# MLP up projection in passes of 512 and 256 columns, block pairs emptied together, partial sums combined in the last group

## The chip, the cores and the metric

The kernel runs on one core of a Trainium2 chip. The metric is the time of one execution on the device in microseconds (us). TensorE is called PE here, VectorE DVE, ScalarE ACT, GpSimd POOL and SyncE SP.

## What is computed

The reference is a trunk of two layers over 256 positions of width 2048, in float32. Each layer adds an attention mixer and an MLP to the residual stream; the change is in the MLP:

```python
def squared_relu_mlp(h, w_up, w_down):
    return jnp.square(jax.nn.relu(h @ w_up)) @ w_down

for layer in range(DEPTH):
    ...
    h = rms_norm(x, mlp_norm[layer])
    x = x + squared_relu_mlp(h, w_up[layer], w_down[layer]).astype(x.dtype)
```

`w_up` is 2048 x 8192 and `w_down` 8192 x 2048.

## The kernel before

Every weight is multiplied in two parts, `hi` (rounded to the matmul's type) and `lo` (the rest); the moving or stationary activations have such parts too, and a product takes three matmuls: hi with hi, hi with lo, lo with hi.

All weights pass through one list, `stream`, of chunks of 128 x 1024 (some 128 x 512). SP loads `raw` tiles of 1 MB (three buffers), ACT copies a chunk to `hi` (L1276, five buffers), DVE makes `lo` = raw - hi (L1284, four buffers), and PE uses both. The main loop does, for chunk i: issue `hi` up to i + 4, `lo` up to i + 3, the matmuls of chunk i, and then a tick of `Jobs`, a list of generators that issue the work beside the stream; a job asks at each `yield` for the tick of its next step. Every engine runs its own instructions in the order in which this loop issues them, so the loop's order is each engine's queue. A tick follows an up or down chunk, and the second chunk of a pair of product chunks.

An MLP (`mlp`) has eight groups of 1024 hidden columns. The up projection of a group is four blocks of 256 columns, each of four chunks: a step (one of 16 k tiles, one half of the block) is three 256-wide matmuls into the PSUM tile `up` (L463 to L465). `up_done` empties a block: Relu from PSUM (L1000), Square into `hr` (L1002), and, as a job one tick later, four sums and differences (L1011 to L1014), ACT's copy into `hs` (L1015) and DVE's rest (L1016), the seven operands of a Strassen product.

The down projection of groups 0 to 6 is done as seven products (L496 to L498) into the PSUM tiles `s0` and `s1`. A unit of 1 MB gives four chunks: a plain one, a single one of half the size, and two that DVE prepares first, w13 (L1043) and w24 (L1049, L1050). Per group there are 32 such chunks, and two of them go with one up chunk of the next group. `products_done` copies the seven sums to `stage` (L1072), and POOL adds them to `sums` in DRAM (L1077). After group 6, `combine` loads them back (L1085), adds them (L1090 to L1095), scales them (L1098), transposes them on PE (L1105) and adds them to the residual `xT` (L1106). The last group's down projection is plain: eight blocks of two chunks (L472, L473), emptied by a copy and three DVE instructions (`down_done`, L1127 to L1131).

Small PE results (transposes, norms) go to `side`, two PSUM banks kept through the whole program.

## Time and profile before

| | |
|---|---|
| median of 3 runs | 2223.57 us (2222.49 to 2226.78) |
| the profiled execution | 2223.32 us, span 2221.5 us |
| PE busy | 2156.0 us (97% of the span) |
| DVE busy | 1745.0 us (79%) |
| ACT busy | 1316.7 us (59%) |
| mean granted PE clock | 0.987 |

The span runs from the first to the last instruction; the execution's time has 1.8 us around it. Matmuls overlap: a row of 0.28 us is followed by the next after some 0.12 us, so the rate is read from the number of matmuls in a stretch, and not from the length of one. "Busy" counts a stretch in which at least one is under way. A granted clock of 1.00 is 2.4 GHz, and 0.50 is 1.2 GHz. The first MLP runs from 361 to 1095 us of the span, the second from 1470 to the end.

### The profile page before, as it was taken

How to read it: one execution, taken by the hardware profiler on the slowest of the kernel's cores; microseconds unless marked ns; L12 is line 12 of the kernel's file. 1: busy time of each engine (PE TensorE's matmuls, PEld its weight loads, DVE VectorE, ACT ScalarE, POOL GpSimd, SP SyncE). 2: the span in 40 equal slices, each digit the busy share in tenths (PEclk: the TensorE clock that was granted, in tenths of full speed). 3: DMA queues.
4: the chain of work that ended last, by engine and by line, in shares of the span. 5: the costliest groups of instructions: out<-in, count | busy, mean ns of one | idle time of the engine just before them, and what ended most of it. 6: DMA issues, size and time to landing. Idle time of an engine off the chain costs nothing.

```text
span 2221.5 us, 39419 instructions
## 1 busy us (share of the span) xinstructions
PE 2156.0 (97%) x16086; PEld 2058.3 (93%) x16086; DVE 1745.0 (79%) x2248; ACT 1316.7 (59%) x1777; POOL 108.9 (5%) x144
## 2 busy tenths in 40 slices
PE   9999999999999999978999999999999999999787
PEld 7898989999999999978888899899999999999776
DVE  6765666898999999977966665568898999999766
ACT  6554545566667666655655446455666666666553
POOL 0000000000000000000000000000000000000000
PEclk9999999999999999999999999999999999999898
DMA  8545456577888888877554456565778888888772
GB/s 264 171 148 161 152 188 177 183 248 216 239 229 246 232 240 240 238 218 227 175 171 136 154 185 191 147 191 179 250 223 241 229 242 235 240 239 233 210 230 83
DMA packets 297685, 455.51 MB, mean 205 GB/s; under 512 B 10696, under 2 KB 172560, under 8 KB 297376
## 3 DMA queue, kind: packets, MB, share of 16 engines
q1 hardware_dynamic: 280224, 392.32, 56.0%
q0 software_dynamic: 17248, 60.67, 13.0%
q8 instruction: 126, 2.06, 0.4%
q14 instruction: 55, 0.45, 0.1%
q10 hardware_dynamic: 32, 0.01, 0.0%
HBM read 399.49 MB, written 53.48 MB: 204 GB/s over the span
## 4 chain that ended last, share of the span: by engine, by line
issue 26%; PE 20%; DMA 2%; POOL 2%; DVE 2%; ACT 1%; POOLq 0%; ACTq 0%; DVEq 0%; SPq 0%
PE mm L472 7%; PE mm L473 4%; POOL sums L1077 2%; PE mm L457 1%; PE mm L458 1%; PE mm L459 1%; DMA sums<-stage 1%; DMA hs<-sums 1%; PE up L463 1%; PE up L464 1%; PE up L465 1%; DVE lo L1284 1%; PE side L350 1%; DMA raw<-w_up 1%; PE mm L475 1%
## 5 line engine op out<-in xcount | busy, mean ns | idle before, releaser
L1284 DVE TENSOR_TENSOR lo<-raw,hi 128x1024 fp32r<-128x1024 f32 (+1 forms) x756 | 825.1, 1113 | 189.2 <-PE mm L473 74.9
L1276 ACT ACTIVATE hi<-raw 128x1024 fp32r<-128x1024 f32 (+1 forms) x756 | 717.9, 966 | 413.8 <-DMA raw<-w_up 169.2
L465 PE MATMUL up<-xs,lo 128*128 128x256 f32 x2048 | 579.6, 283 | 6.6 <-DVE lo L1284 6.2
L463 PE MATMUL up<-xs,hi 128*128 128x256 f32 x2048 | 578.8, 283 | 1.6 <-DVE xT L757 1.6
L464 PE MATMUL up<-xs,hi 128*128 128x256 f32 x2048 | 579.0, 283 | 0.0
L496 PE MATMUL s<-hi,hs 128*128 128x256 f32 x1568 | 445.7, 284 | 0.0
L497 PE MATMUL s<-lo,hs 128*128 128x256 f32 x1568 | 444.1, 283 | 0.0
L498 PE MATMUL s<-hi,hs 128*128 128x256 f32 x1568 | 443.7, 283 | 0.0
L465 PEld LDWEIGHTS up<-xs,lo 128*128 128x128 f32 x2048 | 387.8, 189 | 12.0 <-DVE lo L1284 11.2
L463 PEld LDWEIGHTS up<-xs,hi 128*128 128x128 f32 x2048 | 385.2, 188 | 1.9 <-ACT hi L1276 1.9
L464 PEld LDWEIGHTS up<-xs,hi 128*128 128x128 f32 x2048 | 385.0, 188 | 0.0
L472 PE MATMUL mm<-xs,hi 128*128 128x512 f32 x885 | 319.5, 401 | 0.4 <-ACT hi L1276 0.4
L1276 ACT ACTIVATE hi<-w 128x1024 fp32r<-128x1024 f32 x224 | 236.1, 1054 | 130.3 <-DVE w L1050 85.6
L496 PEld LDWEIGHTS s<-hi,hs 128*128 128x128 f32 x1568 | 300.1, 191 | 0.0
L497 PEld LDWEIGHTS s<-lo,hs 128*128 128x128 f32 x1568 | 300.1, 191 | 0.0
L498 PEld LDWEIGHTS s<-hi,hs 128*128 128x128 f32 x1568 | 299.5, 191 | 0.0
L1284 DVE TENSOR_TENSOR lo<-w,hi 128x1024 fp32r<-128x1024 f32 x224 | 273.8, 1222 | 24.2 <-ACT hi L1276 18.9
L473 PE MATMUL mm<-xs,lo 128*128 128x256 f32 x944 | 259.3, 280 | 0.2 <-DVE lo L1284 0.2
L472 PEld LDWEIGHTS mm<-xs,hi 128*128 128x128 f32 x885 | 166.1, 188 | 38.1 <-ACT hi L1276 0.9
L473 PEld LDWEIGHTS mm<-xs,lo 128*128 128x128 f32 x944 | 177.5, 188 | 3.0 <-DVE lo L1284 0.5
L1043 DVE TENSOR_TENSOR w<-raw 128x1024 f32<-128x1024 f32 x112 | 136.4, 1218 | 0.0
L1077 POOL DMA_DIRECT2D sums<-stage x96 | 82.9, 863 | 973.0 <-ACT stage L1072 955.8
(302 smaller groups left out, 2669.9 us busy)
## 6 DMA issues: line engine op xcount, KB each, us to landing
raw<-w_up SPq DMA_DIRECT2D x128, 1024.0 KB, 5.8
raw<-w_down SPq DMA_DIRECT2D x128, 1024.0 KB, 6.4
raw<-od_w_in SPq DMA_DIRECT2D x36, 1024.0 KB, 5.0
raw<-ev_w_in SPq DMA_DIRECT2D x30, 1024.0 KB, 5.3
sums<-stage POOLq DMA_DIRECT2D x56, 512.0 KB, 6.1
sums<-stage POOLq DMA_DIRECT2D x56, 384.0 KB, 6.4
raw<-ev_w_out SPq DMA_DIRECT2D x16, 1024.0 KB, 5.0
raw<-od_w_in SPq DMA_DIRECT2D x20, 512.0 KB, 4.4
```

The costliest lines, as they stand in the source:

```text
L463: mm(ps[:, j], hi[:, n, c], m[:, 0:T], start=first and j == 0, stop=False)
L464: mm(ps[:, j], hi[:, n, c], m[:, T:], start=False, stop=False)
L465: mm(ps[:, j], lo[:, n, c], m[:, 0:T], start=False, stop=last and j == 1)
L472: mm(ps[:, j], hi[:, n, c], m, start=first, stop=False)
L473: mm(ps[:, j, 0:T], lo[:, n, c], m[:, 0:T], start=False, stop=False)
L496: mm(ps, x[:, a, 0:P], hi[:, o, q], start=first and at % 2 == 0, stop=False)
L497: mm(ps, x[:, a, 0:P], lo[:, o, q], start=False, stop=False)
L498: mm(ps, x[:, a, P:], hi[:, o, q], start=False, stop=last and (at % 2 == 1 or prod == 3))
L1043: tt(four(t), w[:, :, :, 1].rearrange("p q k c -> p k q c"), w[:, :, 0].rearrange("p q h c -> p h q c"), op=OP.subtract)
L1077: nc.gpsimd.dma_start(to, stage, accum_op=OP.add)
L1276: act(d, r, AF.Copy)
L1284: tt(d, r, f32(h), op=OP.subtract)
```

## The change

- A step of the up projection is one 512-wide matmul of `hi` with both parts of the activations, and one 256-wide of `lo`, as in the mixers. The block has a PSUM tile of two banks; ACT copies the second half out, and DVE adds the first to it, ahead of Relu.
- Up weights are loaded 512 columns wide, four k tiles at a time; two blocks share a load and alternate chunk by chunk.
- The two blocks of a pair have one `hr` and one `hs` tile. The four sums, the copy and the rest are issued once for both, the sums in the tick of the second block, the copy and the rest one tick later.
- The up projection runs 18 chunks ahead of the products instead of 16; the last two pairs of product chunks have no up chunk behind them.
- All four `combine` start when the last product is done, and their transposes stand between the blocks of the last down projection.
- The two `side` banks are kept by the mixers alone. In an MLP such results go to halves of `s0` and `s1`, and later of `up`. The final norm's gain is loaded late, into the tiles of w13 and w24.

```diff
     def side():
-        return psum.tile([P, 512], F32, name="side", bufs=2)
+        return st["side"]()
...
     def open_banks(pool_ctx, name):
-        st["banks"] = pool_ctx.enter_context(
+        pool = st["banks"] = pool_ctx.enter_context(
             tc.tile_pool(name=name, bufs=1, space=bass.MemoryType.PSUM, reuse_waits="tile"))
+        st["side"] = lambda: pool.tile([P, 512], F32, name="side", bufs=2)
...
             c = slice(j * P, (j + 1) * P)
-            if block.kind == "U":
-                mm(ps[:, j], hi[:, n, c], m[:, 0:T], start=first and j == 0, stop=False)
-                mm(ps[:, j], hi[:, n, c], m[:, T:], start=False, stop=False)
-                mm(ps[:, j], lo[:, n, c], m[:, 0:T], start=False, stop=last and j == 1)
-            elif block.kind == "last":
+            if block.kind == "last":
...
         def open_pool():
             open_banks(pool_ctx, f"mlp{layer}_ps")
+            turn = [0]
+
+            def free_half():
+                turn[0] ^= 1
+                return banks(f"s{turn[0]}", 1)[:, 0]
+            st["side"] = free_half
             E["pool"] = pool_ctx.enter_context(tc.tile_pool(name=f"mlp{layer}", bufs=1, reuse_waits="tile"))
-            if last:
-                fn = E["fn"] = E["pool"].tile([P, D], F32, name="fn")
-                nc.gpsimd.dma_start(fn, final_norm.unsqueeze(0).to_broadcast([P, D]))
+
+        def load_gain():
+            fn = [E["pool"].tile([P, D // 2], F32, name=n) for n in ("w13", "w24")]
+            for i in range(2):
+                c = slice(i * D // 2, (i + 1) * D // 2)
+                nc.gpsimd.dma_start(fn[i], final_norm[c].unsqueeze(0).to_broadcast([P, D // 2]))
+            E["fn"] = lambda c0, n: fn[c0 // (D // 2)][:, c0 % (D // 2):c0 % (D // 2) + n]
...
         def take_up():
-            return st["banks"].tile([P, 2, T], F32, name="up", bufs=2)
+            return banks("up", 2)
         def take_down(b):
             return lambda: banks(f"s{b % 2}", 1)
         def take_last():
-            two = [take_up(), take_up()]
-            return [t[:, 0] for t in two]
+            ps = banks("s1", 1)
+            return [ps[:, j, 0:T] for j in range(2)]
         def up_done(grp, b):
             def f(ps):
                 t = temp()
-                act(t, ps, AF.Relu)
-                r = E["pool"].tile([P, 8, P], F32, name="hr", bufs=1)
-                act(r[:, 0:4].rearrange("p (j k) t -> p j (k t)", j=2), t, AF.Square)
-
-                def job():
-                    h = E["pool"].tile([P, 7, 2 * P], F32R, name="hs", bufs=2 * nb)
-                    if grp == NGRP - 1:
-                        h = h.rearrange("p o t -> p (o t)")[:, 0:4 * T].rearrange("p (j t) -> p j t", j=2)
-                        split_into(h, r[:, 0:4].rearrange("p (j k) t -> p j (k t)", j=2))
-                    else:
-
-                        tt(r[:, 4], r[:, 0], r[:, 2], op=OP.add)
-                        tt(r[:, 6], r[:, 1], r[:, 0], op=OP.subtract)
-                        tt(r[:, 5], r[:, 4], r[:, 1], op=OP.subtract)
-                        tt(r[:, 7], r[:, 3], r[:, 5], op=OP.subtract)
-                        act(h[:, :, 0:P], r[:, 1:8], AF.Copy)
-                        tt(h[:, :, P:], r[:, 1:8], f32(h[:, :, 0:P]), op=OP.subtract)
-                    hs[grp, b] = h
-                    jobs.done.add(("h", layer, grp, b))
+                act(t, ps[:, :, T:], AF.Copy)
+                tt(t, ps[:, :, 0:T], t, op=OP.add)
+                act(t, t, AF.Relu)
+                if b % 2 == 0:
+                    E["r"] = E["pool"].tile([P, 2, 8, P], F32, name="hr", bufs=1)
+                r = E["r"]
+                act(r[:, b % 2, 0:4].rearrange("p (j k) t -> p j (k t)", j=2), t, AF.Square)
+                if b % 2:
+                    jobs.spawn(job(r), keys=[("h", layer, grp, i) for i in (b - 1, b)], delay=0)
+
+            def job(r):
+                h = E["pool"].tile([P, 2, 7, 2 * P], F32R, name="hs", bufs=nb)
+                if grp == NGRP - 1:
                     yield 1, 0
-                jobs.spawn(job(), keys=[("h", layer, grp, b)], delay=1)
+                    for i in range(2):
+                        hi = h[:, i].rearrange("p o t -> p (o t)")[:, 0:4 * T].rearrange("p (j t) -> p j t", j=2)
+                        split_into(hi, r[:, i, 0:4].rearrange("p (j k) t -> p j (k t)", j=2))
+                        hs[grp, b - 1 + i] = hi
+                else:
+
+                    tt(r[:, :, 4], r[:, :, 0], r[:, :, 2], op=OP.add)
+                    tt(r[:, :, 6], r[:, :, 1], r[:, :, 0], op=OP.subtract)
+                    tt(r[:, :, 5], r[:, :, 4], r[:, :, 1], op=OP.subtract)
+                    tt(r[:, :, 7], r[:, :, 3], r[:, :, 5], op=OP.subtract)
+                    yield 1, 0
+                    act(h[:, :, :, 0:P], r[:, :, 1:8], AF.Copy)
+                    tt(h[:, :, :, P:], r[:, :, 1:8], f32(h[:, :, :, 0:P]), op=OP.subtract)
+                    for i in range(2):
+                        hs[grp, b - 1 + i] = h[:, i]
+                for i in range(2):
+                    jobs.done.add(("h", layer, grp, b - 1 + i))
+                yield 1, 0
             return f
...
-                if grp == NGRP - 2 and half == "s1":
-                    jobs.spawn(combine(cb), keys=[("sum", cb)], delay=1)
+                if grp == NGRP - 2 and half == "s1" and cb == 3:
+                    st["side"] = lambda: banks("up", 2)[:, 0]
+                    for i in range(4):
+                        jobs.spawn(combine(i), keys=[("sum", i)], delay=i)
+                    if last:
+                        load_gain()
             return f
         def combine(cb):
-            s = E["pool"].tile([P, 7, 2 * P], F32, name="hs", bufs=2 * nb)
+            if cb % 2 == 0:
+                E["s"] = E["pool"].tile([P, 2, 7, 2 * P], F32, name="hs", bufs=nb)
+            s = E["s"][:, cb % 2]
             nc.gpsimd.dma_start(s, sums[cb].rearrange("p (o c) -> p o c", o=7))
-            yield 3, 0
...
-            r = E.setdefault("r", st["r"])
+            r = E.setdefault("rms", st["r"])
             for tok in range(2):
                 act(g[:, tok], g[:, tok], AF.Copy, scale=r[:, tok:tok + 1])
-            yield 1, 1
+            yield 2, 1
...
         def up_list(grp):
-            blocks = [Block("U", eights(up, grp * W + b * T, KT), mov, up_done(grp, b), take=take_up)
-                      for b in range(nb)]
-            return [(block, i) for block in blocks for i in range(len(block.chunks))]
+            order = []
+            for b in range(0, nb, 2):
+                c = w_chunks(up, grp * W + b * T, fours(KT))
+                two = [Block("T", c[i], mov, up_done(grp, b + i), take=take_up) for i in range(2)]
+                order += [(block, i) for i in range(len(c[0])) for block in two]
+            return order
...
-        stream.extend(up_list(0))
-        for grp in range(NGRP - 1):
-            s, u = product_list(grp), up_list(grp + 1)
-            for i in range(len(u)):
-                stream.extend(s[2 * i:2 * i + 2] + u[i:i + 1])
+        ups = [c for grp in range(NGRP) for c in up_list(grp)]
+        prods = [c for grp in range(NGRP - 1) for c in product_list(grp)]
+        lead = KT // 4 * nb + 2
+        stream.extend(ups[:lead])
+        for i in range(len(prods) // 2):
+            stream.extend(prods[2 * i:2 * i + 2] + ups[lead + i:lead + i + 1])
```

How the rows move on the engines is shown at the end of an up block (DVE, ACT) and in the last groups (PE). First DVE at the end of an up block beside products, before: the block's last matmul was issued just ahead of the row of w24 with L1049, and `lo` rows from there are the chunks of w13, of w24, of the next up chunk and of the plain and single chunks behind it.

```order
L1049 TENSOR_TENSOR w24_8304<-w13_8270,raw_8080 128x512 [waits DVE_49]
L1050 TENSOR_TENSOR w24_8304<-raw_8080,w24_8304 128x512 [waits DVE_49]
L1284 TENSOR_TENSOR lo_8308<-w13_8270,hi_8269 128x1024 [waits PE_49,Activation_49]
L1284 TENSOR_TENSOR lo_8325<-w24_8304,hi_8303 128x1024 [waits PE_49,Activation_49]
L1011 TENSOR_TENSOR hr_8301<-hr_8301 128x128
L1012 TENSOR_TENSOR hr_8301<-hr_8301 128x128
L1013 TENSOR_TENSOR hr_8301<-hr_8301 128x128 [waits DVE_49]
L1014 TENSOR_TENSOR hr_8301<-hr_8301 128x128 [waits DVE_49]
L1016 TENSOR_TENSOR hs_8335<-hr_8301,hs_8335 128x7x128 [waits Activation_49]
L1284 TENSOR_TENSOR lo_8344<-raw_8193,hi_8323 128x1024 [waits PE_49]
```

DVE had no row in emptying the block, and its sums follow the `lo` of w13 and w24 by a tick. DVE now, from the end of the second block of a pair on:

```order
L1007 TENSOR_TENSOR t_8008<-up_7654,t_8008 128x512 [waits Activation_49]
L1026 TENSOR_TENSOR hr_7951<-hr_7951 128x2x128 [waits Activation_49]
L1027 TENSOR_TENSOR hr_7951<-hr_7951 128x2x128
L1028 TENSOR_TENSOR hr_7951<-hr_7951 128x2x128 [waits DVE_49]
L1029 TENSOR_TENSOR hr_7951<-hr_7951 128x2x128 [waits DVE_49]
L1066 TENSOR_TENSOR w24_8019<-w13_7987,raw_7818 128x512
L1067 TENSOR_TENSOR w24_8019<-raw_7818,w24_8019 128x512 [waits DVE_49]
L1311 TENSOR_TENSOR lo_8023<-w13_7987,hi_7986 128x1024
L1311 TENSOR_TENSOR lo_8039<-w24_8019,hi_8018 128x1024 [waits PE_49,Activation_49]
L1032 TENSOR_TENSOR hs_8013<-hr_7951,hs_8013 128x14x128 [waits Activation_49]
L1311 TENSOR_TENSOR lo_8056<-raw_7917,hi_8037 128x1024 [waits PE_49]
```

The add of the block (L1007) and the four sums of the pair (L1026 to L1029) now stand ahead of w24 and of the `lo` of w13; the `hs` row is twice as long and comes, as before, between the `lo` of w24 and that of the next up chunk.

ACT now, at the same place (L1006 is the new copy out of PSUM, L1008 Relu, L1012 Square, L1031 the copy for both blocks):

```order
L1006 ACTIVATE t_8008<-up_7654 128x512 [waits PE_49]
L1008 ACTIVATE t_8008<-t_8008 128x512 [waits DVE_49]
L1012 ACTIVATE hr_7951<-t_8008 128x512 [waits Activation_49]
L1303 ACTIVATE hi_8018<-w24_8019 128x1024 [waits DVE_49]
L1303 ACTIVATE hi_8037<-raw_7917 128x1024 [waits PE_49]
L1089 ACTIVATE stage_8049<-s0_7900 128x768 [waits DMASW5_49,PE_49]
L1031 ACTIVATE hs_8013<-hr_7951 128x14x128 [waits Activation_49]
```

Relu waits for DVE's add, the `hi` of w24 stands behind Square and waits for DVE's w24, and the stage copy stands ahead of the long copy.

The second place is PE in the last groups of an MLP. Before, the first transposes of a `combine` (here the first of layer 1) stand behind an up chunk, with products to follow:

```order
L464 MATMUL up<-xs,hi 128x256
L465 MATMUL up<-xs,lo 128x256
L1105 MATMUL side<-misc,hr 128x128 x4
L496 MATMUL s_22729<-hi,hs 128x256
L497 MATMUL s_22729<-lo,hs 128x256
```

Now they stand behind the third block of the last down projection:

```order
L469 MATMUL s_21473<-hs,lo 128x256
L471 MATMUL s_21473<-hs,hi 128x512
L1128 MATMUL up<-misc,hr 128x128 x4
L468 MATMUL s_21538<-hs,hi 128x512
L469 MATMUL s_21538<-hs,lo 128x256
```

They have moved behind all products and six down chunks, and write to a tile of `up`.

## Rows read from the trace of the kernel before

**Rows 1.** The page: busy us (share of the span) and instructions.

```profile
PE 2156.0 (97%) x16086; PEld 2058.3 (93%) x16086; DVE 1745.0 (79%) x2248; ACT 1316.7 (59%) x1777; POOL 108.9 (5%) x144
```

**Rows 2.** Stretches: us, busy us (x instructions) by engine, PEclk, DMA, GB/s.

```profile
300.00:330.00 30.00, 30.00 (x173) 26.14 (x173) 18.52 (x21) 14.02 (x17) 0.00 (x0) 1.00 0.61 201
669.00:930.00 261.00, 260.88 (x2182) 260.19 (x2181) 239.11 (x279) 177.92 (x207) 20.71 (x24) 1.00 0.85 238
```

**Rows 3.** Stretches at the end of the two MLPs, same columns.

```profile
952.00:1042.00 90.00, 73.73 (x564) 72.35 (x563) 66.35 (x81) 48.66 (x58) 7.69 (x10) 0.91 0.72 210
2066.00:2151.00 85.00, 66.23 (x507) 64.72 (x507) 60.64 (x74) 42.66 (x50) 6.35 (x9) 0.88 0.68 199
```

**Rows 4.** The waits of PE: total us, times, longest.

```profile
PE side L1105 <- ACT hr L1098: 43.1, 9, 7.6
PE up L465 <- DVE lo L1284: 6.2, 13, 1.6
```

**Rows 5.** Timeline of DVE at a block's end: start, us, instruction, idle before.

```profile
800.92 0.69 DVE L1049 TENSOR_TENSOR w<-w,raw 128x512 f32<-128x512 f32 x1
...
802.25 1.22 DVE L1284 TENSOR_TENSOR lo<-w,hi 128x1024 fp32r<-128x1024 f32 x1
803.74 1.23 DVE L1284 TENSOR_TENSOR lo<-w,hi 128x1024 fp32r<-128x1024 f32 x1 [0.28 <-ACT hi L1276]
804.89 0.28 DVE L1011 TENSOR_TENSOR hr<-hr 128x128 f32<-128x128 f32 x1
805.09 0.28 DVE L1012 TENSOR_TENSOR hr<-hr 128x128 f32<-128x128 f32 x1
...
805.61 0.29 DVE L1014 TENSOR_TENSOR hr<-hr 128x128 f32<-128x128 f32 x1
806.98 1.09 DVE L1016 TENSOR_TENSOR hs<-hr,hs 128x896 fp32r<-128x896 f32 x1 [1.08 <-ACT hs L1015]
807.99 1.22 DVE L1284 TENSOR_TENSOR lo<-raw,hi 128x1024 fp32r<-128x1024 f32 x1
```

**Rows 6.** Timeline of ACT at the same place.

```profile
801.50 0.59 ACT L1000 ACTIVATE t<-up 128x512 f32<-128x512 f32 x1
802.12 0.64 ACT L1002 ACTIVATE hr<-t 128x512 f32<-128x512 f32 x1
802.66 1.04 ACT L1276 ACTIVATE hi<-w 128x1024 fp32r<-128x1024 f32 x1
...
805.99 0.95 ACT L1015 ACTIVATE hs<-hr 128x896 fp32r<-128x896 f32 x1 [1.34 <-DVE hr L1014]
```

**Rows 7.** Timeline of PE at the same place.

```profile
801.24 0.28 PE L496 MATMUL s<-hi,hs 128*128 128x256 f32 x1
...
803.38 0.28 PE L463 MATMUL up<-xs,hi 128*128 128x256 f32 x1
...
806.25 0.28 PE L496 MATMUL s<-hi,hs 128*128 128x256 f32 x1
```

**Rows 8.** The tile up: count, ns min/median/max, first and last start.

```profile
L465 PE MATMUL up<-xs,lo x2048: 274/282/389, 361.4 to 2151.8; 128*128 128x256 f32 x187
...
L1207 DVE TENSOR_TENSOR t<-up,rB x2: 414/415/416, 2209.0 to 2209.8; 128x256 f32<-128x256 f32 x2
```

**Rows 9.** A stretch of layer 0's last stage, columns as in 2.

```profile
1072.00:1078.00 6.00, 6.00 (x37) 5.24 (x36) 5.93 (x10) 4.21 (x8) 0.00 (x0) 1.00 0.68 220
```

**Rows 10.** The page, DMA issues: count, KB each, us to landing.

```profile
sums<-stage POOLq DMA_DIRECT2D x56, 384.0 KB, 6.4
```

**Rows 11.** Groups of ACT by form: busy us, mean ns, idle before.

```profile
L1072 ACT ACTIVATE stage<-s 128x768 f32<-128x768 f32 x56 | 44.4, 792 | 0.0
```

**Rows 12.** Timeline of PE before a combine's transpose in layer 0.

```profile
1028.76 0.33 PE L1105 MATMUL side<-misc,hr 128*128 128x128 f32 x1 [3.65 <-ACT hr L1098]
```

**Rows 13.** Stretches around an idle of PE, columns as in 2.

```profile
545.00:548.40 3.40, 1.87 (x16) 1.67 (x15) 2.32 (x4) 2.42 (x3) 0.00 (x0) 1.00 0.85 258
1029.00:1033.00 4.00, 3.72 (x20) 3.63 (x20) 3.81 (x6) 1.84 (x3) 0.00 (x0) 0.57 0.02 4
```

More of the change, by code (lines that the diff above doesn't have):

```diff
@@ L142, in trunk @@
     tmp = ctx.enter_context(tc.tile_pool(name="tmp", bufs=1))
-    psum = ctx.enter_context(tc.tile_pool(name="psum", bufs=1, space=bass.MemoryType.PSUM))
     dram = ctx.enter_context(tc.tile_pool(name="dram", bufs=1, space=bass.MemoryType.DRAM))
@@ L1077, in f @@
                     nc.gpsimd.dma_start(to, stage, accum_op=OP.add)
[L1078 to L1079 removed]
+                if grp == NGRP - 2 and half == "s1" and cb == 3:
[4 more added lines that the diff above has]
+                        load_gain()
             return f
         def combine(cb):
[L1084 removed]
+            if cb % 2 == 0:
+                E["s"] = E["pool"].tile([P, 2, 7, 2 * P], F32, name="hs", bufs=nb)
+            s = E["s"][:, cb % 2]
             nc.gpsimd.dma_start(s, sums[cb].rearrange("p (o c) -> p o c", o=7))
[L1086 removed]
+            yield 4 + cb, 0
             p1, p2, p3, p5, p7, p6, p4 = (s[:, i] for i in range(7))
@@ L1195, in job @@
                     nc.tensor.transpose(pv[:, tok, j * P:(j + 1) * P], xT[b][:, j, tok * P:(tok + 1) * P], ident)
-            fn = E["fn"][:, b * T:(b + 1) * T]
+            fn = E["fn"](b * T, T)
             tt(st["o"][:, :, b * T:(b + 1) * T], pv, fn[:, None, :].to_broadcast([P, 2, T]), op=OP.mult)
@@ L1209, in last_block @@
             act(sq[:, j], xl[:, j], AF.Square)
-        sums, turn = banks("s1", 1), side()
+        sums, turn = banks("s0", 1), side()
         def add_up(a, first, last):
@@ L1220, in turn_out @@
             tt(o[:, :, c0:c0 + P], turn[:, j * T:(j + 1) * T].rearrange("p (t c) -> p t c", c=P),
-               E["fn"][:, None, c0:c0 + P].to_broadcast([P, 2, P]), op=OP.mult)
+               E["fn"](c0, P)[:, None].to_broadcast([P, 2, P]), op=OP.mult)
         add_up(acc[:, 0], True, False)
```

## The prediction

> **What bounds the kernel now.** I read the engines' busy times first, then stretches of the span, then single instructions around the one place that the change touches most. PE is busy for 2156.0 us of the span and DVE for 1745.0 us [rows 1], so any gain has to come out of PE's own work or its idle time. The stretches say where there is idle time. In the steady part of the first MLP PE is busy 260.88 of 261 us, and 2182 matmuls in that time are 119.6 ns each; DVE is busy 239.11 us (92%) beside it [rows 2]. At the end of each MLP, while the partial sums come back, PE is busy only 73.73 of 90 us and 66.23 of 85 us, at a mean granted clock of 0.91 and 0.88 [rows 3]. All of the kernel's long PE idles stand there: nine waits of the transposes of `combine`, 43.1 us, against 6.2 us in thirteen waits for a `lo` in the up projection [rows 4].
>
> The third view is the end of one up block in that steady part [rows 5 to 7]. Call T the start of the matmul behind the block's last one, 801.24. PE then has a plain and a single product chunk (to 803.38, 2.14 us), an up chunk (to 806.25, 2.87 us), the chunks of w13 and w24 (24 matmuls, 2.87 us) and the next up chunk, whose first `lo` matmul it reaches at about 809.12 + 0.24 = 809.36. DVE meanwhile makes the `lo` of w13 (802.25) and w24 (803.74), four `hr` sums, waits 1.08 us for ACT's copy, makes `hs` (806.98) and then the `lo` of that up chunk, from 807.99 to 809.21. It is done 0.15 us ahead of PE. **PE loses nothing there, but the cover is used up**: whatever is put into DVE's queue between T and that `lo` is paid by PE. That is what the change does.
>
> **The change part by part.** *Matmuls of the up projection.* 2048 steps of three 256-wide matmuls [rows 8] become one of 512 and one of 256. Three cost 3 x 119.6 = 359 ns. The pair stands in the first output projection: 173 matmuls in 30 us [rows 2], 347 ns a pair. 12 ns x 2048 = **24 us less**. The Trainium skill (TensorE: Matmul & The Clock Gate, section Back-to-back issue gap) puts the gap at N/2.4 GHz plus about 2.5 ns; an estimate by it saves one such 2.5 ns a step, 5 us in all, and the sum would be 19 us higher. By that rule the trace does not agree: 119.6 ns stand against its 109, and the measurement decides.
>
> *Sums combined in the last group.* Before, the four transposes of a `combine` follow its DMA by three ticks, and PE waits up to 7.6 us [rows 4]. Now all four start when the last product is done and the first transposes stand behind three blocks of the down projection (the order pieces of PE), some 17 us later. What goes is the idle of the two stretches, 16.3 + 18.8 us, and what the matmuls there ran slower: 73.73 us for 564 against 564 x 0.1196 = 67.5, and 66.23 for 507 against 60.6, together 11.9. **47 us less.**
>
> What comes instead is DVE work in the down blocks. There DVE was already at 5.93 of 6 us in layer 0 [rows 9]. In layer 1 the last stage took from 2151.8 to the tail at 2209.0, 57.2 us [rows 8]. Behind its first block (6.5 us) DVE now has 11 splits of 1.14 us, 21 instructions of the down sums, 8 sums into xT, 7 squares and 7 outputs at about 0.65 us (0.69 in rows 5, started 0.08 us before the end of the one ahead), and four combines of 2.5 us: 12.5 + 28 + 10 = 50.5, and 2 to 3 us of waits for transposes. That is 60 us: 3 more. Layer 0 gets 4 more by the same count, with its splits of xs for the outputs. **7 us more**; bounds 0 and 15. The gain loads and the four loads of sums on POOL's queue land about 6 us after their issue [rows 10], and DVE comes to the first some 14 us after the last product, so I price them at nothing; without that cover DVE would wait those 6 us once.
>
> *The end of a pair of up blocks* (the order pieces of DVE and ACT). New per block are a copy of half the PSUM tile on ACT and an add on DVE ahead of Relu; the four sums, the copy and the split are now made for two blocks at once, right in the tick of the second block. DVE takes its queue in order, so at the second block's T it goes: add, four sums, two for w24, `lo` of w13, `lo` of w24, `hs`, `lo` of the up chunk. From rows 5 and 6: ACT starts 0.26 us behind T, DVE 0.04 behind ACT, ACT 0.09 behind DVE, an independent instruction 0.08 before the end of the one ahead. Doubled operands cost twice less one start (twice 0.69 against 1.22 on DVE, twice 0.59 to 0.64 against 1.04 on ACT): 0.4 for a sum, 2.0 for `hs`, 1.7 for the copy.
>
> Copy 0.73 to 1.32 (ACT has the `hi` of w13 ahead of it; 0.26 at the earliest), add to 2.05, Relu to 2.77, Square to 3.43: DVE stands idle from 2.05 to 3.47, since its next row needs Square. Four sums to 5.0, w24 to 6.35, `lo` of w13 from 6.27 to 7.49. PE needs this one at 2.14 + 8 x 0.347 + 0.12 = 5.04: **it waits 2.5 us.** ACT goes on with `hi` of w24 (needs DVE's 6.35) to 7.49, `hi` of the up chunk to 8.45, the stage copy (0.79 [rows 11]) to 9.15, the copy to 10.78; DVE makes `hs` to 12.85 and the `lo` of the up chunk to 13.99. PE, restarted at 7.5, has 1.3 + 1.4 + 0.23 us of work and stands at 10.5: **it waits 3.5 us more.** 6.0 us a pair. With every choice the other way (copy at 0.26, stage behind, smaller starts) it is 4.8. Twelve pairs a layer (groups 1 to 6) run beside products: 24 x 6.0 = **144 us more**. The two pairs of group 0 run among up chunks alone, 2.78 us each, and are covered. The two of the last group have no sums and split a tick later: the same chain gives 1.2 us each, **5 us** in all.
>
> *The clock.* An idle of 3.65 us [rows 12] was followed by a half-rate stretch: mean clock 0.57 over 4 us, where 20 matmuls took 3.72 us of busy time instead of 2.4 [rows 13]. In the stretch from 545 PE was idle for 1.53 of 3.4 us, and the clock stayed at 1.00 [rows 13]. Mine of 3.5 us is nearest to the first, so I take its 1.3 us for each pair: **31 us more**. Ends: 0, and 82 us (3.4 us each, a stretch twice as long, no idle in it).
>
> *At nothing:* up loads with rows twice as long (same bytes; PE's long waits are on ACT and DVE, not on DMA [rows 4]); PSUM side banks gone, since the halves they now come from are free before the products begin and the up banks after the last up chunk. Without that cover PE would wait for the emptying of a bank, a copy and an add, 1.3 us, at each of four phase changes.
>
> **Sum.** Against the profiled execution, 2223.3 us (0.01% under the median shown): - 24 - 47 + 7 + 144 + 5 + 31 = **2339 us**.
>
> **The rivals.** *A, faster:* the chain at the pair's end is covered, and only the gains stay: 2223.3 - 24 - 47 + 7 = 2159 us. For it: the same waits of DVE on ACT stand at every block now and cost PE nothing, DVE has 8% spare and so no lack of work time. It decides below 2.5 us a pair ((2223.3 - 2159 - 5) / 24). Against it: 0.15 us of cover, and an add of three engine changes in an in-order queue ahead of a `lo` that PE needs 5 us after T. *B, half the stall:* the first wait is hidden, because ACT and DVE start earlier than I lay them out, and only 3.5 us stand, without the clock: 2308 - 24 x 2.5 = 2248. *C, the clock falls for the long stretch at every pair*: 2308 + 82 = 2390, and up to 2430 if the 2.5 us idle counts as well. For it, the idles in rows 3, up to 7.6 us, lowered the mean clock to 0.88; against it, mine are shorter.
>
> **How the numbers follow.** My forecast with its bounds (4.8 to 6.5 us a pair, clock 0 to 82) spans 2270 to 2390 and gets 0.70; A 0.13 and the ground between it and now 0.03; B 0.08; C 0.06. 2270 to 2390 alone is too little, so the range goes down to take in B: 2235 to 2400, which leaves A, its border and most of C outside, 2 in 10. Within 0.2% (4.4 us, about what a measurement can tell from no change) lies only that border: 0.03. Faster 0.13, slower 0.84.
>
> **What would show it.** Right: in the steady part PE's busy share falls to about 88%, PE's waits for DVE's `lo` rise from 6 us to over 100, half in the first `lo` matmul of a product chunk and half in an up chunk, at a spacing of about 48 us; DVE waits for ACT at its new add and at the sums; the transposes of the combines wait 1 to 3 us; an up step takes 347 ns. Wrong: PE still busy 99% there (A), or idles of only one kind (B).

## The result and the profile after

The changed kernel takes 2351.95 us (median), against 2225.18 us for the kernel before on the same chip: a ratio of 1.0566, 95% interval 1.0546 to 1.0587. Three of its four executions took 2349.15 to 2353.40 us; the fourth, at a mean granted clock of 0.59, took 3317.65 us and counts in the median, but not in the ratio. The change makes the kernel slower by 127 us; 2339 was forecast. The profiled execution took 2350.5 us, its span 2348.7.

The engines' busy times on the page, to be read beside [rows 1]:

```profile
PE 2187.7 (93%) x14038; PEld 1985.1 (85%) x14038; DVE 1775.9 (76%) x2172; ACT 1355.2 (58%) x1813; POOL 109.4 (5%) x145
```

PE has 2048 matmuls fewer and is busy 32 us longer. Part of that is the clock, whose mean fell from 0.987 to 0.969: in a half-rate stretch the trace has the 256-wide matmuls of the products 0.21 us apart instead of 0.12. How large that part is was not worked out. The waits of PE in the changed kernel (engine, line, waited for: us in total, times, longest), to be read beside [rows 4]:

```profile
PE up L469 <- DVE lo L1311: 54.2, 28, 3.2
PE s L493 <- DVE lo L1311: 52.9, 24, 2.7
PE up L1128 <- ACT hr L1121: 22.5, 10, 5.8
PE up L1222 <- DVE xs L1224: 6.2, 2, 5.6
PE up L1128 <- DVE xT L1129: 4.7, 4, 1.8
PE side L253 <- DVE acc L247: 3.7, 1, 3.7
```

The 6.2 us of waits for a `lo` became 107.1: 24 in a product chunk, 28 in an up chunk. The transposes' 43.1 us became 22.5, and 14.6 us stand in the three rows behind them, which the kernel before did not have. Stretches, columns as in [rows 2]: the steady part, and from the first down matmul to the next stage in each MLP:

```profile
669.00:930.00 261.00, 239.92 (x1595) 221.19 (x1595) 218.03 (x230) 165.47 (x188) 19.03 (x22) 0.96 0.75 212
1082.40:1153.80 71.40, 56.19 (x289) 47.13 (x289) 54.36 (x85) 34.12 (x52) 5.89 (x12) 0.90 0.55 170
2257.00:2334.30 77.30, 58.83 (x327) 50.62 (x328) 55.45 (x83) 28.17 (x39) 4.94 (x8) 0.87 0.45 142
```

PE is busy 239.92 us of the same 261 in which it was busy 260.88, and DVE 218.03 instead of 239.11: neither is short of work time; they wait for each other. The pairs' ends are as regular as forecast: the first waits of neighbouring pairs stand 48 us apart (748.75 and 796.93). One pair's end, first DVE (start, us, instruction, idle before):

```profile
742.62 0.69 DVE L1007 TENSOR_TENSOR t<-up,t 128x512 f32<-128x512 f32 x1 [0.54 <-ACT t L1006]
744.67 0.43 DVE L1026 TENSOR_TENSOR hr<-hr 128x256 f32<-128x256 f32 x1 [1.36 <-ACT hr L1012]
...
747.47 2.43 DVE L1311 TENSOR_TENSOR lo<-w,hi 128x1024 fp32r<-128x1024 f32 x2
751.91 2.03 DVE L1032 TENSOR_TENSOR hs<-hr,hs 128x1792 fp32r<-128x1792 f32 x1 [2.00 <-ACT hs L1031]
753.85 2.95 DVE L1311 TENSOR_TENSOR lo<-raw,hi 128x1024 fp32r<-128x1024 f32 x3
```

and PE, from the first matmul behind the block (T) on:

```profile
741.37 0.28 PE L492 MATMUL s<-hi,hs 128*128 128x256 f32 x1
...
748.75 0.38 PE L493 MATMUL s<-lo,hs 128*128 128x256 f32 x1 [2.13 <-DVE lo L1311]
...
755.12 0.39 PE L469 MATMUL up<-xs,lo 128*128 128x256 f32 x1 [1.70 <-DVE lo L1311]
755.35 0.39 PE L468 MATMUL up<-xs,hi 128*128 128x512 f32 x1
...
757.45 0.39 PE L468 MATMUL up<-xs,hi 128*128 128x512 f32 x1
```

The sums start at T + 3.30 (forecast 3.47), PE has the `lo` of w13 at T + 7.38 (7.49) and that of the up chunk at T + 13.75 (13.99). Six up steps take 2.10 us, 350 ns each (347). The Trainium skill (TensorE: Matmul & The Clock Gate, Back-to-back issue gap) gives N/2.4 GHz plus 2.5 ns for an isolated matmul, an estimate of 325 ns for the two; in this stream the trace does not agree with it.

The clock, in the same place:

```profile
746.00:750.00 4.00, 1.86 (x15) 1.62 (x14) 3.87 (x5) 2.41 (x3) 0.00 (x0) 1.00 0.28 68
750.00:754.00 4.00, 3.42 (x16) 2.92 (x14) 2.09 (x2) 4.00 (x5) 0.86 (x1) 0.57 1.03 269
```

The half-rate stretch follows the first idle and lies between the two. In the down blocks the DMA issues (count, KB each, median us to landing; before: `hs<-sums` 7.4, `raw<-w_down` 6.4) and the chain that ended last (start, us, what) read:

```profile
raw<-w_down SPq DMA_DIRECT2D x128, 1024.0 KB, 7.1
hs<-sums POOLq DMA_DIRECT2D x8, 896.0 KB, 13.1
```

```profile
1087.59 19.47 DMA raw<-w_down
```

Three of the four loads of sums are issued from 1087.19 to 1088.37 and the fourth at 1095.76; a load of `w_down` issued among them lands after 19.47 us. ACT then waits for it, DVE for ACT, and the transposes for both:

```profile
1107.15 2.01 ACT L1303 ACTIVATE hi<-raw 128x1024 fp32r<-128x1024 f32 x2 [5.26 <-DMA raw<-w_down]
```

```profile
1115.71 1.52 PE L1128 MATMUL up<-misc,hr 128*128 128x128 f32 x4 [5.77 <-ACT hr L1121]
```

### The profile page after: what moved, and what is told of

Same layout as the page of the kernel before. It is cut to its first block, busy times and chain, and to the rows that moved or that the text cites. A ratio compares the mean times of both kernels' runs of the same rounds, so it can differ in the third digit from the quotient of the medians.

```text
span 2348.7 us, 35292 instructions
## 1 busy us (share of the span) xinstructions
PE 2187.7 (93%) x14038; PEld 1985.1 (85%) x14038; DVE 1775.9 (76%) x2172; ACT 1355.2 (58%) x1813; POOL 109.4 (5%) x145
## 4 chain that ended last, share of the span: by engine, by line
PE 49%; issue 31%; DVE 7%; ACT 6%; DMA 5%; POOL 2%; DVEq 0%; POOLq 0%; ACTq 0%; SPq 0%
PE mm L468 13%; PE up L468 7%; PE mm L469 7%; PE up L469 4%; DMA raw<-w_up 3%; ACT hi L1303 2%; PE s L492 2%; PE s L493 2%; PE s L494 2%; DVE lo L1311 2%; PE mm L457 2%; PE mm L459 2%; PE mm L458 2%; POOL sums L1094 2%; DMA raw<-w_down 1%
## 5 line engine op out<-in xcount | busy, mean ns | idle before, releaser
L468 PE MATMUL up<-xs,hi 128*128 128x512 f32 x1920 | 697.8, 400 | 1.6 <-DVE xT L753 1.6
L469 PE MATMUL up<-xs,lo 128*128 128x256 f32 x2048 | 571.5, 284 | 54.2 <-DVE lo L1311 54.2
L493 PE MATMUL s<-lo,hs 128*128 128x256 f32 x1568 | 456.3, 291 | 52.9 <-DVE lo L1311 52.9
L494 PE MATMUL s<-hi,hs 128*128 128x256 f32 x1568 | 453.3, 289 | 0.0
L492 PE MATMUL s<-hi,hs 128*128 128x256 f32 x1568 | 453.2, 289 | 0.0
L468 PEld LDWEIGHTS up<-xs,hi 128*128 128x128 f32 x1920 | 366.8, 191 | 78.7 <-ACT hi L1303 1.9
L493 PEld LDWEIGHTS s<-lo,hs 128*128 128x128 f32 x1568 | 309.2, 197 | 60.3 <-DVE lo L1311 57.8
L492 PEld LDWEIGHTS s<-hi,hs 128*128 128x128 f32 x1568 | 309.2, 197 | 7.5
L494 PEld LDWEIGHTS s<-hi,hs 128*128 128x128 f32 x1568 | 309.8, 198 | 0.0
L1089 ACT ACTIVATE stage<-s 128x768 f32<-128x768 f32 x112 | 100.9, 901 | 2.2 <-PE s L494 2.1
L1032 DVE TENSOR_TENSOR hs<-hr,hs 128x1792 fp32r<-128x1792 f32 x28 | 56.7, 2025 | 52.0 <-ACT hs L1031 52.0
```

Source lines behind the costliest of these rows:

```text
L468: mm(ps[:, j], hi[:, n, c], m, start=first, stop=False)
L469: mm(ps[:, j, 0:T], lo[:, n, c], m[:, 0:T], start=False, stop=False)
L492: mm(ps, x[:, a, 0:P], hi[:, o, q], start=first and at % 2 == 0, stop=False)
L493: mm(ps, x[:, a, 0:P], lo[:, o, q], start=False, stop=False)
L494: mm(ps, x[:, a, P:], hi[:, o, q], start=False, stop=last and (at % 2 == 1 or prod == 3))
L1032: tt(h[:, :, :, P:], r[:, :, 1:8], f32(h[:, :, :, 0:P]), op=OP.subtract)
```

## The experiments

Two theories stood at the start. Queue theory: PE loses what stands in DVE's and ACT's queues between a block's end and the next `lo`, so order and place decide. Work theory: the engines have too much to do, and order only moves the wait. All runs in one table: the median, the ratio to the kernel before on the same chip with its interval, the time from the first up matmul to the first down matmul of each MLP ("products"), and from there to the next stage (in layer 1 to the last down matmul).

| kernel | us | ratio | products 0, 1 | down 0, 1 |
|---|---|---|---|---|
| before | 2225 | 1 | 681.2, 681.6 | 53.0, 55.7 |
| changed | 2352.0 | 1.0566 | 721.0, 721.0 | 71.4, 77.4 |
| late_sums | 2336.8 | 1.0494 (1.0463 to 1.0524) | 714.7, 716.4 | 70.8, 76.8 |
| unpaired | 2339.0 | 1.0504 (1.0473 to 1.0534) | 714.0, 720.5 | 70.6, 75.9 |
| p256_unp | 2317.6 | 1.0407 (1.0377 to 1.0438) | 703.9, 708.4 | 69.9, 76.4 |
| lo5_late | 2587.9 | 1.1622 (1.1588 to 1.1655) | 840.4, 840.8 | 71.0, 77.5 |
| serial | 2301.3 | 1.0345 (1.0324 to 1.0366) | 698.2, 697.9 | 69.4, 77.2 |
| serial_p256 | 2250.2 | 1.0111 (1.0090 to 1.0132) | 673.4, 673.1 | 69.8, 74.7 |
| serial_lead16 | 2210.8 | 0.9942 (0.9921 to 0.9963) | 657.1, 658.7 | 69.6, 71.7 |
| zero_mm | 2343.3 | 1.0535 (1.0511 to 1.0559) | 719.4, 718.5 | 69.9, 77.9 |
| gated | 2354.8 | 1.0582 (1.0560 to 1.0605) | 726.8, 724.8 | 68.6, 74.3 |
| comb_only | 2216.5 | 0.9943 (0.9923 to 0.9962) | 659.1, 656.8 | 69.4, 74.0 |
| late_turn | 2181.2 | 0.9795 (0.9766 to 0.9823) | 660.1, 659.2 | 49.1, 54.6 |
| serial_la | 2500.9 | 1.1228 (1.1206 to 1.1250) | 796.1, 795.8 | 74.8, 77.7 |

**late_sums.** The pair's sums one tick later.

```diff
-                    jobs.spawn(job(r), keys=[("h", layer, grp, i) for i in (b - 1, b)], delay=0)
+                    jobs.spawn(job(r), keys=[("h", layer, grp, i) for i in (b - 1, b)], delay=1)
...
-                    yield 1, 0
                     act(h[:, :, :, 0:P], r[:, :, 1:8], AF.Copy)
```

> The pair's four sums are issued one tick later, behind the lo of w13, in the tick of the copy and the split; nothing else. Queue theory (PE loses at a pair's end because the lo of w13 and then the lo of the next up chunk stand behind the pair's rows in DVE's queue): the wait in front of the lo of w13 (52.9 us in 24 in the changed kernel) shrinks to under 10 us, since only add, w24 and that lo are left, but the sums now stand ahead of the lo of the next up chunk, which is ready some 12 us after the block's last matmul where PE can reach it after 8: that wait grows from 54 us to 80 to 110, one idle a pair in place of two. Time 2325 to 2355 us, the clock still about 0.97. Rival (the sums' place is what costs; taken out of the way, PE is free again): both waits fall, time under 2270 us. Rival (the amount of DVE and ACT work, not its order): no wait moves, 2350 us.

```profile
PE up L469 <- DVE lo L1309: 102.0, 28, 3.9
```

The wait in the product chunk is gone and the other grew from 54.2 to 102.0, 3.9 us at every pair. Order decides where PE waits, as the queue theory has it, and the time, 2336.8 us, lies in the range expected.

**unpaired.** `hr` and `hs` for each block; as before the change, the sums, the copy and the rest of a block come one tick behind its end.

```diff
-                    E["r"] = E["pool"].tile([P, 2, 8, P], F32, name="hr", bufs=1)
+                r = E["pool"].tile([P, 8, P], F32, name="hr", bufs=2)
...
-                h = E["pool"].tile([P, 2, 7, 2 * P], F32R, name="hs", bufs=nb)
+                    h = E["pool"].tile([P, 7, 2 * P], F32R, name="hs", bufs=2 * nb)
...
```

> Each block has hr and hs of its own again, with its sums, copy and split one tick later, as before the change; passes, loads, lead and combines as in the changed kernel. Queue theory: behind a block DVE has the add, w24, lo of w13, lo of w24, four sums of one block, the split of one block and then the lo of the next up chunk; that one is some 2 us late at every block (48 a phase instead of 24 pairs), the first wait (lo of w13) is gone. About 1 to 2 us for each of 48 blocks and little of the half clock, since idles are shorter: 2250 to 2310 us. Rival (paired operands are harmless, the new passes with their copy and add cost it all): 2335 to 2365 us, as the changed kernel. Rival (pairing costs it all): under 2230 us.

```profile
PE up L469 <- DVE lo L1300: 97.9, 54, 3.3
PE s L493 <- DVE lo L1300: 18.2, 25, 0.8
```

116.1 us of waits in place of 107.1, in 79 pieces instead of 52, and 13 us less in all. The time expected missed, and the rival held that paired operands are harmless: without pairs about the same waits stand at the ends of single blocks.

**p256_unp.** Also passes of 256 columns, emptied by Relu from PSUM.

```diff
-                act(t, ps[:, :, T:], AF.Copy)
-                tt(t, ps[:, :, 0:T], t, op=OP.add)
-                act(t, t, AF.Relu)
+                act(t, ps, AF.Relu)
...
```

> As the one without pairs, and the up projection is again three 256-wide matmuls a step into one bank, emptied by Relu straight from PSUM: no copy, no add. What stays of the change is loads 512 wide, the lead of 18 chunks, the combines in the last group and the side banks. Queue theory: the steady part is that of the kernel before (no waits for lo above some 10 us in all, clock 0.99 or more there, the first MLP's product part about 634 us), so the time is 2225 less what the combines in the last group save: the 47 us of idle and slow matmuls at the ends of the products, less the 40 us or so by which the last stages are longer in the changed kernel: 2205 to 2225 us. Rival (512-wide up loads or the lead cost something themselves): product parts above 640 us and over 2235 us in all.

```profile
PE up L465 <- DVE lo L1302: 74.2, 49, 3.0
```

A clear miss: copy, add and pairs are all gone, and 74.2 us of waits stay. What is left of the change there is the order of the up blocks with its wider loads, the lead, the moved combines and the banks; order, lead and banks I had held for harmless.

**serial_p256.** As p256_unp, but loads of 256 columns and the four blocks one behind the other.

```diff
-            order = []
-            for b in range(0, nb, 2):
-                c = w_chunks(up, grp * W + b * T, fours(KT))
-                two = [Block("U", c[i], mov, up_done(grp, b + i), take=take_up) for i in range(2)]
-                order += [(block, i) for i in range(len(c[0])) for block in two]
-            return order
+            blocks = [Block("U", eights(up, grp * W + b * T, KT), mov, up_done(grp, b), take=take_up)
+                      for b in range(nb)]
+            return [(block, i) for block in blocks for i in range(len(block.chunks))]
```

> Against the run with passes of 256 and no pairs (2317.6 us) one thing is changed: the up weights are loaded 256 columns wide again and the four blocks of a group follow each other, so that block ends lie four up chunks apart, and not two in adjacent up chunks. Lead of 18, combines in the last group and side banks stay as in the changed kernel. Theory (alternating blocks put two block ends side by side, and DVE, which has 0.15 us of cover at one end, is late at both): the 49 waits for the lo of an up chunk (74.2 us) fall below 10 us, the half-rate stretches beside the products go, lead and product part of the first MLP together take 655 to 665 us (703.9 in that run, 681.2 before, which had the idles of the combines in it), time 2205 to 2230 us. Rival (the lead of 18 chunks moved the block ends against the product chunks, and alternation is harmless): the waits stay at 60 us or more, 2290 us or more.

```profile
PE up L465 <- DVE lo L1299: 37.9, 43, 1.8
```

67 us faster (2317.6 to 2250.2): with blocks alternating chunk by chunk over one load, two blocks end in neighbouring up chunks, and their rows on DVE stand behind one another. The run takes back the wider loads too, so the 67 us are of the two together. Half of the waits stay, so both theories of that run hold in part.

**serial_lead16.** The same with the lead of before.

```diff
-        lead = KT // 4 * nb + 2
+        lead = KT // 4 * nb
```

> The run with 256-wide passes and blocks in sequence (2250.2 us, 37.9 us of waits for the lo of up chunks), with a lead of 16 chunks instead of 18; side banks and combines stay as in the changed kernel. Lead theory (two chunks more move the block ends, and the loads behind them, against the product chunks and their sums): the waits for lo fall to about 10 us, as in the run with the combines alone moved, and the first MLP's lead and product part go from 673.4 to 656 to 662 us: 2210 to 2225 us. Rival (the side banks in up and s tiles, or the hr buffers, make the waits): 35 us or more of waits, 2243 to 2255 us.

```profile
PE up L465 <- DVE lo L1299: 10.8, 26, 1.2
```

Another 39 us. ACT at a block's end with the lead of 18 (L1010 is the Relu of the block):

```profile
691.79 1.06 ACT L1291 ACTIVATE hi<-raw 128x1024 fp32r<-128x1024 f32 x1 [3.71 <-DMA raw<-w_up]
692.76 1.04 ACT L1291 ACTIVATE hi<-w 128x1024 fp32r<-128x1024 f32 x1
693.71 0.58 ACT L1010 ACTIVATE t<-up 128x512 f32<-128x512 f32 x1
```

and with 16:

```profile
689.88 1.06 ACT L1291 ACTIVATE hi<-raw 128x1024 fp32r<-128x1024 f32 x1 [1.25 <-DMA raw<-w_up]
690.85 1.01 ACT L1082 ACTIVATE stage<-s 128x1024 f32<-128x1024 f32 x1
691.75 1.05 ACT L1291 ACTIVATE hi<-w 128x1024 fp32r<-128x1024 f32 x1
692.69 0.59 ACT L1010 ACTIVATE t<-up 128x512 f32<-128x512 f32 x1
```

With 18 the wait for a load of `w_up` just ahead of a block's end is 3.71 us, with 16 it is 1.25. Over the whole program ACT's waits for these loads (us in total, times, longest) are fewer and longer with 18, but in sum they are shorter than with 16:

```profile
ACT hi L1291 <- DMA raw<-w_up: 179.8, 59, 5.7
ACT hi L1291 <- DMA raw<-w_up: 198.2, 91, 5.3
```

That the lead is the cause is shown; that it works through the place of these waits is read from the two traces, and no run changes that alone. p256_unp, serial_p256 and serial_lead16 have the same rows on DVE in the products, and the waits for `lo` of an up chunk went from 74.2 to 37.9 and 10.8 us by order, loads and lead: queue theory holds here, work theory does not.

**serial.** As serial_p256 (lead of 18), but with passes of 512 and 256, and so with copy and add.

```diff
-                act(t, ps, AF.Relu)
+                act(t, ps[:, :, T:], AF.Copy)
+                tt(t, ps[:, :, 0:T], t, op=OP.add)
+                act(t, t, AF.Relu)
...
```

> As the last, but with the passes of 512 and 256 columns and so the copy and the add at every block's end: against the unpaired run (2339.0 us) only the order of the blocks and the width of the loads differ. Alternation theory: block ends lie apart, and only copy and add (0.7 us of DVE, and its wait for ACT's copy, against 0.15 us of cover) come into the queue of one block: 0.7 to 1.7 us a block, 48 blocks, 34 to 80 us of waits at the lo of an up chunk, less 24 us for the passes: 2225 to 2275 us, slower than with 256-wide passes. Rival (copy and add, not the order, make the waits of 98 us): waits stay over 90 us, 2320 us or more. Rival (copy and add are covered once the blocks lie apart): 2185 to 2205 us, faster than with passes of 256.

```profile
PE up L469 <- DVE lo L1297: 82.2, 56, 2.3
```

51 us slower than serial_p256: 44 us more of waits for `lo`, in spite of cheaper matmuls. Copy and add are not covered even where blocks end apart. At 2301.3 us the run lies above the 2275 that was expected at most, and its 82.2 us of waits lie under the 90 that the rival asked for (copy and add alone make the waits).

**lo5_late and serial_la.** Two tries to buy cover: one more `lo` buffer in the MLPs, issued one chunk sooner (with late sums); and one more `hi` and `lo` each, both one chunk sooner (on serial, `hr` with one buffer).

```diff
-            los[i] = wts.tile([P, 1024], F32R, name="lo", bufs=LO_BUFS)
+            los[i] = st["xlo"]() if extra(i) else wts.tile([P, 1024], F32R, name="lo", bufs=LO_BUFS)
...
-        lo_to(i + LO_BUFS)
+        lo_to(lo_ahead(i))
...
```

> The sums are late as in the first run, and in the MLPs a fifth lo buffer is there, with the lo of a chunk issued one chunk sooner (four chunks ahead of its matmuls instead of three). Queue theory: the lo of the next up chunk then stands ahead of the pair's split in DVE's queue, and the lo behind it has a chunk more of cover: the two waits (54.2 and 52.9 us) fall to under 25 us in all, the half-rate stretches behind each pair go with them, and the clock is 0.99 or more in the steady part. Time 2170 to 2215 us, against 2352. Rival (DVE and ACT are short of work time; order and look-ahead only move the waits): the waits keep 80 us or more in all, time 2310 us or more. Rival (waits go but the half clock stays, so it isn't caused by them): about 2240 to 2270 us.

```profile
DVE lo L1320 <- ACT hi L1302: 454.6, 401, 5.0
ACT hi L1302 <- DVE w L1059: 231.4, 100, 3.3
```

> The run with passes of 512 and 256 columns and blocks in sequence (2301.3 us, 82.2 us of waits for the lo of up chunks), with one more hi and one more lo buffer in the MLPs and both issued one chunk further ahead; hr has one buffer again. The earlier run with one more lo alone (2587.9 us) put the lo of a chunk directly behind its hi, and DVE waited 454.6 us for ACT; here the distance of the two is what it was. Cover theory (the copy and the add at a block's end cost because DVE has 0.15 us of cover there; one chunk more is 1.4 to 2.9 us): the waits for lo fall below 20 us, and the product parts from 647 to 610 to 625 us: 2225 to 2255 us. Rival (DVE is short of work time, 0.7 us more a block on 92%): the waits keep 50 us or more, 2275 us or more.

```profile
DVE lo L1309 <- ACT hi L1301: 278.0, 122, 5.1
ACT hi L1301 <- DMA raw<-w_up: 255.7, 47, 6.9
```

Both expectations fell, and by far. In the first, the `lo` of a chunk stands directly behind its `hi`, so DVE waits for ACT at every chunk. In the second the distance is kept, but ACT waits for loads of `w_up` for 255.7 us (141.9 in serial) and DVE for ACT. Why looking further ahead makes the loads late is not settled; a fourth `raw` buffer was not tried.

**zero_mm.** Matmuls of zeros in both idles of a pair; they add zero. The cut shows the first of the two places.

```diff
+                for _ in range(16 if fill else 0):
+                    mm(ps, zeros[:, 0:P], zeros[:, 0:T], start=False, stop=False)
                 mm(ps, x[:, a, 0:P], lo[:, o, q], start=False, stop=False)
```

> The changed kernel, with matmuls of zeros put where PE waits at a pair's end beside products (16 of 256 columns ahead of the first lo of w13, 7 of 512 ahead of the first lo of the next up chunk); they add zero to the sums. Clock theory (each pair's two idles of 2.1 and 1.6 us are followed by a half-rate stretch of 3.4 us, which costs 1.3 to 1.8 us of its own): the idles are filled, the half-rate stretches beside the products go, the clock there is 1.00, and 24 pairs give back 30 to 43 us: 2308 to 2325 us. Rival (the half-rate stretch lies in time that PE would wait anyway, so the clock costs nothing): 2345 to 2355 us. Rival (the zeros last longer than the idles, 2.2 and 1.7 us): 2360 us or more.

```profile
669.00:930.00 261.00, 248.12 (x1710) 223.69 (x1714) 217.21 (x231) 163.89 (x189) 19.03 (x22) 1.00 0.74 211
```

The clock is 1.00 where it was 0.96, and the products are 1.6 and 2.5 us shorter, not 15 to 20 each. The rival holds, with a total 1.7 us below its range: the half-rate stretch lies in time that PE would wait anyway.

**gated.** The loads of sums two to four held back on POOL, and issued later by one to three ticks; their adds keep their ticks.

```diff
-                        jobs.spawn(combine(i), keys=[("sum", i)], delay=i)
+                        jobs.spawn(combine(i), keys=[("sum", i)], delay=2 * i)
...
+            if cb:
+                nc.gpsimd.tensor_tensor(s[:, 0, 0:2], E["t"][:, 0, 0:2], mhalf, op=OP.add)
             nc.gpsimd.dma_start(s, sums[cb].rearrange("p (o c) -> p o c", o=7))
-            yield 4 + cb, 0
+            yield 4, 0
```

> The changed kernel, with the loads of the second to fourth partial sum held on POOL until the down blocks have reached them (a two-element add on POOL of a tile of the down block), so that the four loads of 0.9 MB no longer start together. Contention theory (the down stages are 18 and 22 us longer than before because the four loads delay the loads of w_down, one of which took 19.5 us): the longest w_down load falls below 12 us, the down stage of each layer falls by 6 to 12 us, time 2328 to 2342 us. Rival (the down stage is longer because of the transposes' waits and DVE's work there): the loads land sooner, but the stage keeps within 3 us of 71 and 77 us, time 2345 to 2355 us. Rival (POOL's wait makes the sums late): the transposes wait more, over 2355 us.

```profile
hs<-sums POOLq DMA_DIRECT2D x8, 896.0 KB, 9.2
```

```profile
1093.39 17.44 DMA raw<-w_down
```

The loads of sums land in 9.2 us instead of 13.1 (medians), and the down stages get 2.8 and 3.1 us shorter. But a load of `w_down` still took 17.44 us, where below 12 was expected, so the collision was only in part taken away, and the run does not tell how much of the longer stages it makes. The products came out 4 to 6 us longer, for which I have no reason, so the total says nothing.

**comb_only.** The kernel before, only with the combines in the last group; as in the changed kernel, their adds and transposes stand more ticks behind the loads.

```diff
-                if grp == NGRP - 2 and half == "s1":
-                    jobs.spawn(combine(cb), keys=[("sum", cb)], delay=1)
+                if grp == NGRP - 2 and half == "s1" and cb == 3:
+                    for i in range(4):
+                        jobs.spawn(combine(i), keys=[("sum", i)], delay=i)
...
-            yield 3, 0
+            yield 4 + cb, 0
...
-            yield 1, 1
+            yield 2, 1
```

> The kernel before, with one part of the change alone: all four combines start when the last product is done, their adds four ticks or more later and the transposes two ticks behind the adds, in the down blocks; the side banks, the lead of 16, the 256-wide loads and passes stay. The forecast's own terms for this part were 47 us less and 7 us more: 2183 us. Theory from the changed kernel's trace (the idles move into the last stages instead of going): product parts of about 613 us in place of 634.5, but last stages 16 to 20 us longer each, as in the run with 256-wide passes and blocks in sequence: 2205 to 2225 us. And if the lead of 18 chunks made the 37.9 us of lo waits in that run, they are under 10 us here; if the moved combines made them, they stay.

The products lose 22.1 and 24.8 us, 46.9 together (forecast 47), and the down stages gain 16.4 and 18.3 (forecast 7 in all). The time, 2216.5 us, lies in the range expected.

**late_turn.** The kernel before, its combines in their place, adds three ticks and transposes one tick later; sums added in place, so that `hr` is not held.

```diff
-            yield 3, 0
+            yield 6, 0
...
-            yield 1, 1
+            yield 2, 1
...
```

> The kernel before, with its combines where they were, but the adds of a combine stand six ticks behind its load instead of three and the transposes two ticks behind the adds instead of one; the sums are added in place in the loaded tile, so that hr is not held. Theory (the 43.1 us of idle before the transposes come from DVE, which stands at its first add until the load has landed, 39.4 us in 8, and the transposes behind it; it is a matter of where the rows stand, not of which group): DVE's wait for the loads falls below 8 us, PE's for the transposes below 12 us, and 30 to 45 us go with nothing given back: 2178 to 2195 us, faster than both kernels. Rival (DVE has no room for the adds in that stretch, and lo comes late instead): PE's waits for lo rise by 20 us or more, 2205 us or more.

DVE's wait at its first add in the kernel before, then what PE waits for the transposes here (43.1 us in [rows 4]):

```profile
DVE t L1090 <- DMA hs<-sums: 39.4, 8, 7.5
```

```profile
PE side L1105 <- DVE xT L1106: 1.5, 1, 1.5
PE side L1105 <- ACT hs L1098: 1.2, 3, 0.6
```

Stretches, columns as in [rows 2]: the steady part here, and from 930 to the last up matmul of the first MLP, before and here:

```profile
669.00:930.00 261.00, 259.91 (x2170) 258.82 (x2169) 237.42 (x278) 175.55 (x204) 20.72 (x24) 1.00 0.84 237
930.00:1042.26 112.26, 96.00 (x749) 94.48 (x748) 86.57 (x104) 63.69 (x76) 9.43 (x12) 0.92 0.74 216
930.00:1021.87 91.87, 90.79 (x756) 89.97 (x755) 84.44 (x102) 61.63 (x74) 8.56 (x11) 1.00 0.92 260
```

About as many matmuls take 91.87 us in place of 112.26, at full clock. The idle before the transposes came from DVE, which in the kernel before stood at its first add until the sums had landed, 39.4 us in 8 times. Asked three ticks later, it has no wait for them, and nothing is given back in the down stages (49.1 and 54.6 us against 53.0 and 55.7): 2181 us, faster than both kernels. The run moves adds and transposes and frees `hr` at once; what each of the three does alone was not tried.

## Why the prediction was right, and where not

Sign and size held, 2351.95 against 2339 in a range of 2235 to 2400, and so did the mechanism: DVE's queue between a block's end and the next `lo` makes PE wait in both places named. Rival A falls with 107 us of waits, B with both waits standing. Of C it is true that the half-rate stretch comes beside the pairs, but not that it costs. By the terms of the forecast:

- *Passes, 24 us less:* 350 ns a step against the forecast 347; 9 ns less than the 359 before, and so 18 us.
- *Idles at the ends, 47 us less:* the products are 46.9 us shorter in comb_only.
- *Pairs, 144 us, and the last group, 5:* PE meets the second `lo` at T + 13.75. Without waits it would be there at T + 7.97 (5.04 and 2.93 by the forecast's own rows), so 5.8 us a pair, 139 in all. Outside those pairs the first MLP has two such waits, of 2.73 us (at 417.69) and 0.85 us (at 1041.54). The split was off, 2.1 and 1.7 us of idle for 2.5 and 3.5, since the half-rate stretch between the idles eats of the second.
- *Clock, 31 us:* this step failed. It was added to the waits, but lies inside them. Against comb_only less 9 us of passes a layer (650 and 648) the products of the changed kernel are 71 and 73 us longer, 144 in all; forecast 144 + 5 + 31 = 180.
- *Down stages, 7 us:* this step failed the other way: 18.4 and 21.7 us, and the odd mixer behind the first is 7 us longer (375.0 to 382.2), 3.7 of it in the wait at L253. I took DVE for busy all through the stage, from six us in which it was busy for 5.93 [rows 9]. Over the two whole stages it was busy 44.11 of 53.02 and 41.43 of 55.65 us before (the rows below). In the changed kernel it is busy 54.36 and 55.45 us, 10 and 14 more, and idle 17 and 22 us, 8 more in each, where I took 2 to 3 us of waits for transposes and priced the loads of sums at nothing. PE waits there for ACT's `hr` for 22.5 us; the longest of these waits, 5.77 us, goes back to the load of `w_down` that took 19.47. How the rest divides between late loads and the order of DVE's rows is open.

DVE is the third engine in the rows of the two stages of the kernel before, columns as in [rows 2]:

```profile
1042.38:1095.40 53.02, 48.37 (x267) 41.70 (x266) 44.11 (x65) 31.33 (x49) 2.58 (x7) 0.94 0.59 180
2151.95:2207.60 55.65, 51.15 (x305) 44.90 (x304) 41.43 (x56) 22.95 (x31) 0.56 (x1) 0.94 0.39 121
```

The measured terms give 2223.3 - 18 - 47 + 144 + 40 + 7 = 2349. The 144 is a difference of two runs, so this sum adds up nearly by its making. Two misses of 36 us (144 for 180) and 40 us (47 for 7) had opposite signs: that the total came within 13 us is in part luck. Two edits had no price in the forecast, the lead of 18 and the alternation of two blocks; they were in the order pieces from which the chain at the pair's end was laid out, and so in its time. In the kernel without copy and add the lead costs 39 us, and the alternation, with its wider loads, 67 on top of it. They, copy and add (51 in serial) and the pairs (13) all draw on the 0.15 us of cover [rows 5], so their prices do not add up to the whole; and the pair, under whose name the forecast put 144 us, is the smallest of the four. What the changed kernel would take with the lead of 16 was not tried.

Of the signs named ahead, the waits over 100 us, half in each place, held. PE's busy share in the steady part is 92%, not 88%, and the transposes wait up to 5.8 us, not 1 to 3.

## What to carry to other kernels

Where DVE reached a tile 0.15 us ahead of PE, the rows that came between were paid by PE (44 us of waits for 48 copies and adds), and so was the move that brought two such places together: price the order and the phase, not only the rows. The idle of an in-order engine that stood at a load was best removed by asking later in the same place; moving the whole step to another stage moved 35 of 47 us with it. A slow clock behind a wait cost next to nothing here, because another wait followed in the same chain.

## What was not expected of the hardware

A load of 1 MB took 19.47 us to land beside loads of 0.9 MB, against a median of 7.1; that these loads are the cause was not shown. And the clock: the pairs of the changed kernel, with idles of 2.1 and 1.7 us, have half-rate stretches as at 750 to 754 and a mean of 0.96 from 669 to 930; serial_p256, whose waits for `lo` are at most 1.8 us, has 0.99 in the same stretch:

```profile
669.00:930.00 261.00, 249.37 (x2058) 247.09 (x2057) 224.86 (x265) 170.66 (x199) 19.90 (x23) 0.99 0.81 224
```
